# A decoder trunk step: weight preparation in spaced steps behind the evictions, rows transposed later, fourteen paired projections instead of thirteen

## The chip, the cores and the metric

The kernel runs on one NeuronCore of a Trainium2 chip. The core has five engines with queues of their own: TensorE (PE in the profile; its weight loads are PEld), VectorE (DVE), ScalarE (ACT), GpSimd (POOL) and SyncE (SP, which here only issues DMAs). The metric is the device time of one execution in microseconds (us); the median of three runs stands for a kernel.

## The reference

One layer of a decoder for a prompt of 1024 tokens and 32 sample tokens (8 sequences of 4), all in float32, model width 1024:

```python
h = layer_norm(ALPHA * x + 0.5 * swiglu(x, f1_w1, f1_w3, f1_w2), ln1_g, ln1_b)
z = h @ w_in + b_in                       # 42 blocks of 128 columns
# 18 blocks q, k, v of three attention groups; 8 blocks u, v of the gMLP; 16 blocks of gates gA, gB
att = combine_groups(...)                 # dilated sliding-window attention, prompt and sample
yb  = u * (tril(W_s) @ LN(v) + b)         # gMLP in chunks of 128
mix = (sigmoid(ga) * (att @ w_oa) + sigmoid(gb) * (yb @ w_ob)) @ w_out
h = layer_norm(ALPHA * h + mix, ln2_g, ln2_b)
h = layer_norm(ALPHA * h + 0.5 * swiglu(h, f2_w1, f2_w3, f2_w2), ln3_g, ln3_b)
```

The sample group also reads a stored key/value state of each window, and the shifted states are outputs.

## The kernel before

**Tiling.** The 1056 tokens lie along the free dimension in four chunks of 264 (C = 264, NC = 4), the 1024 features along eight blocks of 128 partitions. Each float32 operand is split into two parts of a faster format (fp32r): `split` (L253, L254) casts the value to a high part on ACT and subtracts it on DVE for the low part. A product of two such operands is three matmuls (`mm3`, L242): high by high, high by low, low by high. Every matmul of the main work multiplies a 128x128 weight block with 264 columns.

**Plain products and pairs.** A block of 128 output columns can be computed plainly: for one chunk `dense8` runs 8 x 3 = 24 matmuls into one PSUM bank. A gate done so is four calls of `gate8`. Two output blocks can instead be computed together by `pair` with a scheme of seven half-size products (Strassen's, in Winograd's form): the tokens and the features are halved, sums and differences of the input halves are built once by `spread`, and sums of the weight halves are built for each pair by `prep`. Each of the seven products is 24 matmuls over two PSUM banks; they run in the order 1, 2, 6, 7, 5, 4, 3 (called p1, p2, p6, p7, p5, p4, p3 here). So a pair takes 168 matmuls where two plain blocks take 192. After each product its banks are evicted into an SBUF tile: the first contribution by ACT (`put`, L1034), later ones by DVE (`add`, L1043). Banks come back soon: `one` holds p1, then p6, p5 and p3; `three` holds p7, then p4; `two` holds p2.

The feed-forward layers use the same scheme (`hidden`), and their second matrix a scheme of the same seven products with three inner blocks (`seven`).

**Order of the projection stage.** `widen` computes 6 of the 16 gates plainly (NLEAD = 6; the first 3 chunk by chunk while the layer norm before them ends, 3 more afterwards) and then NZ = 13 pairs: nine of q, k, v and four of u, v. The last ten gates are computed in `mix`, beside the attention.

**Preparing a pair's weights** (`prep`, a generator in five steps). Step 1 loads the two weight blocks (`ab`, L376, and `cd`, L377) on SP and splits `ab`. Step 2 builds s12, two sums, on POOL (L386, L387). Step 3 splits s12 into `h12`, `l12` and begins s34 (L392). Step 4 ends s34 (L394) and splits the quarter `dd` of `cd`. Step 5 splits s34. p1 and p2 use `ab`, p6 and p5 use s12, p7 and p3 use s34, p4 uses `dd`. The raw tiles R and the sums Q have two buffers each, so that a load waits for the readers of the pair before. While pair f runs, each product is followed by one step of prep(f+1) and by a `tick`.

**Ticks.** A tick advances generators of background work: three steps of the queue `bg`, one of `slow` (the sample attention, `sample`, and the input sums), three of `mid`. `sample_rows` is in `bg`: after four pauses it transposes on PE the sample tokens of the q, k, v pair before (L1375), copies them by DVE (L1377) and writes them by SP (L1381, L1386). `sample` streams the stored keys and values through three buffers (`M<-kv`, L1406) and multiplies and reduces them on DVE (L1421, L1422, L1432, L1437).

**Who sets the order.** The code is traced once and a list scheduler, with its own estimate of times, then decides each engine's order; each engine runs its list strictly in that order and waits at its head. `urgent` raises the priority of evictions and remembers the last one of each engine; `fenced` makes what is traced under it come after that one on DVE, ACT and SP. Background steps are fenced; the steps of `prep` are not:

```python
            def between():
                if f + 1 in preps:
                    next(preps[f + 1], None)
                self.tick(STEPS["strassen"], 1)
```

Of the kernel before, what the change touches and what calls it, by code (L numbers as in the profile page):

```python
# [59 lines left out]
REST = 3  # L60
GAP = 4
AFTER = 100
LATE = 16
MID = 3
HOP = (4, 1, 4)
# [3 lines left out]
FENCED = (mybir.EngineType.DVE, mybir.EngineType.Activation, mybir.EngineType.SP)  # L69
QKV = [s * 6 + 2 * g + hp for hp, g in HPG for s in range(3)]  # L70
GATES = [*range(34, 42), *range(26, 34)]
NLEAD = 6
NTAIL = 10
LAST = 3
EARLY = 6
BESIDE = {2: 13, 4: 14, 5: 15}
CHUNKED = 3
SPLIT = [*QKV, 22, 23, 24, 25, 18, 19, 20, 21, *GATES[NLEAD : 16 - NTAIL]]
DENSE = GATES[:NLEAD] + GATES[16 - NTAIL :]
# [4 lines left out]
class Trunk:  # L84
# [285 lines left out]
    def prep(self, src, f, H, engine):  # L370

        nc = self.nc
        lo, hi, n = slice(0, H), slice(H, 2 * H), 2 * H
        with self.tc.high_priority(offset=URGENT):
            ab, cd = self.R([P, D])[:, :n], self.R([P, D])[:, :n]
            nc.sync.dma_start(ab, src[1])  # L376
            dma = nc.sync.dma_start(cd, src[0])  # L377
        self.copy_state(dma, 2)
        tt = engine.tensor_tensor
        ah, al = self.W([P, D]), self.W([P, D])  # L380
        self.split(ah[:, :n], al[:, :n], ab)
        if f == LASTW2:
            h34, l34 = self.held([P, D], F32R), self.held([P, D], F32R)
        yield
        s12 = self.Q([P, D])
        tt(s12[:, lo], cd[:, lo], cd[:, hi], op=ALU.add)  # L386
        tt(s12[:, hi], s12[:, lo], ab[:, lo], op=ALU.subtract)  # L387
        yield
        s34 = self.Q([P, D])
        h12, l12 = self.W([P, D]), self.W([P, D])  # L390
        self.split(h12[:, :n], l12[:, :n], s12[:, :n])
        tt(s34[:, lo], ab[:, lo], cd[:, lo], op=ALU.subtract)  # L392
        yield
        tt(s34[:, hi], ab[:, hi], s12[:, hi], op=ALU.subtract)  # L394
        part = lambda h, l, o=0: [((h, l), o + k * P) for k in range(H // P)]
        if n == D:
            dd = self.S([P, D], F32R)
            self.split(dd[:, lo], dd[:, hi], cd[:, hi])
            p4 = part(dd[:, lo], dd[:, hi])
        else:  # L400
            p4 = []
            for h, l, w in ((ah, al, D - n), (h12, l12, H - (D - n))):
                o = H + len(p4) * P
                self.split(h[:, n : n + w], l[:, n : n + w], cd[:, o : o + w])
                p4 += part(h, l, n)[: w // P]
        yield
        if f != LASTW2:
            h34, l34 = self.S([P, D], F32R), self.S([P, D], F32R)
        self.split(h34[:, :n], l34[:, :n], s34[:, :n])
        self.L[f] = {  # L410
            1: part(ah, al), 2: part(ah, al, H), 5: part(h12, l12), 6: part(h12, l12, H),
            7: part(h34, l34), 3: part(h34, l34, H), 4: p4,
        }
        yield

    def product(self, t, p, f, first):
        while any(p not in t for t in self.T):
# [257 lines left out]
    def ffn(self, w13, w2p, w2, i, mode, resid):  # L675
        nc, preps = self.nc, {}
        plain = PLAIN[: 1 if i == 0 else 2]
        blocks = [f for f in range(FB) if f not in plain] + [FB + g for g in range(NG * (KB // 2))]
        after = dict(zip(blocks, blocks[1:]))

        def begin(f):
            if f < FB:
                preps[f] = self.prep(w13[f], f, KH * P, nc.gpsimd if f > 2 else nc.vector)
            else:
                preps[f] = self.prep(w2p[f - FB], f, HP, nc.vector)
            next(preps[f])

        if i == 0:
            self.lns = {}
            self.T, self.L = ({}, {}), {}  # L690
            units = self.lead_in(w13)
            self.new_x(1)
            self.consts()
            s0, s1 = (self.spread(j, self.Y, self.A, self.nc.vector) for j in range(2))
            begin(1)
            with self.tc.high_priority(offset=URGENT):
                for k in range(2):
                    self.load_x(self.nc.sync, 3, k, 0, KH)
            for c, work in enumerate((((2,), s0, s0, 1), ((3,), s0, 1, 1), (s1, s1, s1, 1), (1, s0))):
                self.hidden8(units, 0, c)  # L700
                for x in work:
                    if isinstance(x, tuple):
                        self.new_x(*x)
                    else:
                        next(preps[x] if x == 1 else x, None)
            self.bg.extend((s0, s1))
        else:
            lead, s1 = self.early
            lns, self.lns = self.lns, {}
            self.drain(lns[NC - 2])  # L710
            self.step(self.bg, 1)
            begin(1)
            for c in range(NC):
                self.drain(lns.pop(c))
                if c == NC - 1:
                    self.bg.append(s1)
                    self.step(self.bg, 2)
                for f, u in zip(plain, lead):
                    self.hidden8(u, f, c)
                    if c:  # L720
                        with self.chained():
                            next(preps[1], None)
            lead = self.early = None
        self.sqs = {}
        self.Y = self.A = None
        loads = deque(self.load_sums(resid))
        total = len(loads)

        def ready(f):
            for _ in preps.pop(f):  # L730
                pass
            if f in after:
                begin(after[f])

        def between(f, bg, slow=0):
            if after.get(f) in preps:
                next(preps[after[f]], None)
            self.tick(bg, slow)

        def load(n):  # L740

            with self.tc.high_priority(offset=URGENT):
                while loads and total - len(loads) < n:
                    loads.popleft()()

        for f in blocks[: FB - len(plain)]:
            ready(f)
            if f == FB - 1:
                load(2)
            count = iter(range(1, 8))  # L750

            def step():
                between(f, STEPS["strassen"])
                if f == FB - 1:
                    load(min(HEAD, 2 + 4 * next(count)))

            self.hidden(f, step)
            del self.L[f]
        self.T = ({}, {})
        self.normed = [None] * NC  # L760
        self.out(w2, i, mode, ready, between, load)
# [325 lines left out]
    def widen(self):  # L1087
# [29 lines left out]
        for n in range(CHUNKED, NLEAD):  # L1117
# [3 lines left out]
            for c in (1, 3, 0, 2):  # L1121
                self.gate8(w, DENSE[n], c, AF.Sigmoid, STEPS["lead"], 1)
                if n == NLEAD - 1:
                    next(preps[0], None)
        self.A = None
        for f in range(NZ):
            for _ in preps.pop(f):
# [2 lines left out]
                begin(f + 1)  # L1130

            def between():
                if f + 1 in preps:
                    next(preps[f + 1], None)
                self.tick(STEPS["strassen"], 1)

            self.pair(f, between)
# [231 lines left out]

    def sample_rows(self, *blocks):  # L1370
        nc, a = self.nc, self.a
        yield from self.pause(4)
        p = self.ax_tile()[:NS, : 2 * P].rearrange("p (s x) -> p s x", s=2)
        for x, (_, t) in enumerate(blocks):
            nc.tensor.transpose(p[:, x], t[:, NP:], self.ident)  # L1375
# [533 lines left out]
```

## Time and profile before

| | |
|---|---|
| median of 3 runs | 2154.41 us (2153.32 to 2157.72) |
| the profiled execution's own time | 2154.51 us |
| its span, first to last instruction | 2152.5 us |
| PE busy | 2122.6 us (99%), 17307 matmuls |
| DVE / ACT / POOL busy | 1549.5 (72%) / 889.4 (41%) / 317.1 us (15%) |
| DMA | 426.51 MB, 198 GB/s over the span |
| mean granted TensorE clock | 0.994 |

PE is the engine that is always busy, so the time is the sum of PE's work and of PE's waits. The stages along the span are: first feed-forward layer to about 660 us, its layer norm and the plain gates to about 787 us, the thirteen pairs to 1059 us, `mix` with the attention to about 1480 us, the second feed-forward layer to the end. A busy PE is modelled from pipelined matmuls; the granted clock is a share of 2.4 GHz (0.50 is 1.2 GHz).

### The profile page before, as it was taken

To read this page: it belongs to the slowest core of one execution; us is meant where nothing else is said; L and a number is where in the kernel's file an instruction comes from. 1 tells how busy PE (TensorE), PEld (TensorE's weight loads), DVE (VectorE), ACT (ScalarE), POOL (GpSimd) and SP (SyncE) were. 2 spreads that over 40 slices of the span, in tenths; PEclk is the share of its full clock that TensorE was granted. 3 is DMA by queue.
4 is the path that set the end of the run, shared out by engine and by line. 5 is a ranking of instruction groups with operands and counts; after the bars stand their busy time and mean duration, and the time that the engine had idled before them with its cause. 6 is when DMAs were issued, how large, how long until landed. Compare 5 with 4: busy or idle time off the path is not lost.

```text
span 2152.5 us, 43254 instructions
## 1 busy us (share of the span) xinstructions
PE 2122.6 (99%) x17307; PEld 2085.6 (97%) x17307; DVE 1549.5 (72%) x2727; ACT 889.4 (41%) x1680; POOL 317.1 (15%) x249
## 2 busy tenths in 40 slices
PE   9999999999999999999999999999999999999997
PEld 8999999999999999999988889999999999999997
DVE  8877767747789834777767758787667777657887
ACT  5444444422124634333476544164444444421224
POOL 0432322200000011323000000000323323100000
PEclk9999999999999999999999999999999999999998
DMA  4444555598885335676865765423454554596852
GB/s 155 145 140 170 183 166 168 189 338 315 327 325 176 130 103 177 201 231 198 296 211 187 223 190 177 154 110 110 144 174 156 183 173 153 194 408 267 311 186 81
DMA packets 168377, 426.51 MB, mean 198 GB/s; under 512 B 24352, under 2 KB 59792, under 8 KB 165488
## 3 DMA queue, kind: packets, MB, share of 16 engines
q1 hardware_dynamic: 167744, 423.21, 56.4%
q8 instruction: 135, 2.21, 0.4%
q10 hardware_dynamic: 432, 0.54, 0.1%
q14 instruction: 66, 0.54, 0.1%
HBM read 304.31 MB, written 165.57 MB: 218 GB/s over the span
## 4 chain that ended last, share of the span: by engine, by line
PE 89%; DVE 4%; DMA 4%; POOL 1%; issue 1%; ACT 0%; SPq 0%; ACTq 0%; DVEq 0%; POOLq 0%
PE ax L242 46%; PE mm L242 39%; DMA R<-wz 1%; PE ax L1206 1%; DMA M<-kv 1%; DMA S<-cD 1%; PE ax L1255 1%; PE ax L1232 1%; DVE W L254 1%; DMA S<-hD 0%; DVE S L632 0%; POOL Q L392 0%; POOL Q L387 0%; DVE S L254 0%; PE ax L621 0%
## 5 line engine op out<-in xcount | busy, mean ns | idle before, releaser
L242 PE MATMUL mm<-S,W 128*128 128x264 f32 x5400 | 713.6, 287 | 8.0 <-ACT S L253 2.3
L242 PE MATMUL ax<-S,W 128*128 128x264 f32 x5400 | 708.6, 285 | 1.3 <-ACT S L1034 1.1
L242 PEld LDWEIGHTS mm<-S,W 128*128 128x128 f32 x5400 | 677.1, 189 | 21.0 <-issue 7.0
L242 PEld LDWEIGHTS ax<-S,W 128*128 128x128 f32 x5400 | 678.5, 189 | 4.0 <-ACT S L1034 2.4
L242 PE MATMUL ax<-S,S 128*128 128x264 f32 x3240 | 475.9, 284 | 1.0 <-ACT S L1034 0.5
L242 PEld LDWEIGHTS ax<-S,S 128*128 128x128 f32 x3240 | 427.7, 188 | 1.7 <-DVE S L1043 0.9
L242 PE MATMUL mm<-S,S 128*128 128x264 f32 x2280 | 359.4, 286 | 2.6 <-DVE S L925 2.6
L242 PEld LDWEIGHTS mm<-S,S 128*128 128x128 f32 x2280 | 311.0, 189 | 3.9 <-issue 2.9
L253 ACT CAST W<-R 128x256 fp32r<-128x256 f32 (+2 forms) x175 | 130.6, 764 | 307.5 <-PE mm L242 139.9
L386 POOL TENSOR_TENSOR Q<-R 128x512 f32<-128x512 f32 x49 | 68.1, 1390 | 800.8 <-DMA R<-w13a 198.2
L254 DVE TENSOR_TENSOR W<-R,W 128x256 fp32r<-128x256 f32 (+2 forms) x175 | 154.6, 887 | 23.3 <-ACT W L253 21.7
L253 ACT CAST W<-Q 128x1024 fp32r<-128x1024 f32 (+1 forms) x78 | 76.8, 984 | 217.2 <-POOL Q L387 88.1
L820 DVE SCALAR_TENSOR_TENSOR S<-ax,S 128x264 f32<-128x264 f32 x240 | 99.7, 429 | 66.1 <-PE ax L242 65.7
L462 DVE TENSOR_TENSOR S<-ax,M 128x264 f32<-128x264 f32 x82 | 32.6, 433 | 144.7 <-PE ax L242 144.7
L254 DVE TENSOR_TENSOR S<-Q,S 128x1024 fp32r<-128x1024 f32 (+1 forms) x78 | 113.6, 1456 | 5.5 <-ACT S L253 5.4
L110 POOL CAST S<-ones 128x1 fp32r<-128x1 f32 x36 | 12.5, 355 | 675.7 <-PE ax L242 226.0
L254 DVE TENSOR_TENSOR W<-Q,W 128x1024 fp32r<-128x1024 f32 (+1 forms) x78 | 90.6, 1161 | 29.6 <-ACT W L253 29.6
L253 ACT CAST S<-Q 128x1024 fp32r<-128x1024 f32 (+1 forms) x78 | 76.7, 984 | 68.4 <-PE ax L242 49.8
L254 DVE TENSOR_TENSOR S<-S,M 128x528 fp32r<-128x528 f32 x72 | 84.6, 1175 | 2.5 <-ACT M L253 0.7
L253 ACT CAST S<-R 128x512 fp32r<-128x512 f32 (+1 forms) x62 | 42.0, 677 | 98.9 <-DMA sumsA<-S 40.6
L387 POOL TENSOR_TENSOR Q<-Q,R 128x512 f32<-128x512 f32 x49 | 81.0, 1653 | 2.7
L394 POOL TENSOR_TENSOR Q<-R,Q 128x512 f32<-128x512 f32 x49 | 79.7, 1627 | 1.2
(209 smaller groups left out, 2042.5 us busy)
## 6 DMA issues: line engine op xcount, KB each, us to landing
ws<-st SPq DMA_DIRECT2D x144, 256.0 KB
S<-sumsA SPq DMA_DIRECT2D x63, 528.0 KB
S<-sumsB SPq DMA_DIRECT2D x63, 528.0 KB
M<-kv SPq DMA_DIRECT2D x96, 256.0 KB
sumsA<-M SPq DMA_DIRECT2D x90, 264.0 KB
sumsB<-M SPq DMA_DIRECT2D x90, 264.0 KB
R<-w13b SPq DMA_DIRECT2D x44, 512.0 KB
R<-w13a SPq DMA_DIRECT2D x42, 512.0 KB
```

The source lines that it names most:

```text
L110: self.nc.gpsimd.tensor_copy(t[:, 0, :1] if len(shape) == 3 else t[:, :1], self.ones[:, :1])
L242: mm = lambda a, b, s, e: nc.tensor.matmul(o, a[:, cc], b, start=s, stop=e, skip_group_check=True)
L253: a = self.nc.scalar.copy(hi, src)
L254: b = self.nc.vector.tensor_tensor(lo, src, hi.bitcast(F32), op=ALU.subtract)
L386: tt(s12[:, lo], cd[:, lo], cd[:, hi], op=ALU.add)
L387: tt(s12[:, hi], s12[:, lo], ab[:, lo], op=ALU.subtract)
L394: tt(s34[:, hi], ab[:, hi], s12[:, hi], op=ALU.subtract)
L462: go(one, 5, False, lambda x: tt(h[:, x, 1], one[x], p7[:, x], op=ALU.add))
L820: nc.vector.scalar_tensor_tensor(y(x, r, e), bank[x], HALF, y(x, r, e), op0=ALU.mult, op1=ALU.add)
L1206: m = nc.tensor.matmul(pS[h][:, r, :nk], q[e, i * P : (i + 1) * P], k[e, k0 : k0 + nk], start=True, stop=True)
L1232: nc.tensor.transpose(pT[r][:, h, o], s[:, r, h, o], self.ident)
L1255: nc.tensor.matmul(pv[0][e, (i % 4) * P : (i % 4 + 1) * P], V[:, i - (nb - 1) + b, e], sT[:, r, h, b * P : b * P + P], start=b == 0, stop= ...
```

## The change

NLEAD goes from 6 to 4: two gates (blocks 38 and 39) are no longer computed plainly in `widen` but make a fourteenth pair after the u, v pairs; BESIDE, which names three of the gates left for `mix` by their place in the list, moves by two accordingly. In `prep` the split of `ab` goes from step 1 to step 2, the split of s12 from step 3 to step 4, and the two halves of s34 stand in steps 3 and 4. All steps of `prep` between products are now fenced (`advance`), in the pairs as in the feed-forward layers. `sample_rows` pauses for eight steps instead of four.

```diff
@@ -60,6 +60,7 @@
 REST = 3
 GAP = 4
 AFTER = 100
+ROWS = 8
 LATE = 16
 MID = 3
 HOP = (4, 1, 4)
@@ -69,11 +70,11 @@
 FENCED = (mybir.EngineType.DVE, mybir.EngineType.Activation, mybir.EngineType.SP)
 QKV = [s * 6 + 2 * g + hp for hp, g in HPG for s in range(3)]
 GATES = [*range(34, 42), *range(26, 34)]
-NLEAD = 6
+NLEAD = 4
 NTAIL = 10
 LAST = 3
 EARLY = 6
-BESIDE = {2: 13, 4: 14, 5: 15}
+BESIDE = {2: 11, 4: 12, 5: 13}
 CHUNKED = 3
 SPLIT = [*QKV, 22, 23, 24, 25, 18, 19, 20, 21, *GATES[NLEAD : 16 - NTAIL]]
 DENSE = GATES[:NLEAD] + GATES[16 - NTAIL :]
@@ -377,20 +378,20 @@
             dma = nc.sync.dma_start(cd, src[0])
         self.copy_state(dma, 2)
         tt = engine.tensor_tensor
-        ah, al = self.W([P, D]), self.W([P, D])
-        self.split(ah[:, :n], al[:, :n], ab)
         if f == LASTW2:
             h34, l34 = self.held([P, D], F32R), self.held([P, D], F32R)
         yield
         s12 = self.Q([P, D])
         tt(s12[:, lo], cd[:, lo], cd[:, hi], op=ALU.add)
         tt(s12[:, hi], s12[:, lo], ab[:, lo], op=ALU.subtract)
+        ah, al = self.W([P, D]), self.W([P, D])
+        self.split(ah[:, :n], al[:, :n], ab)
         yield
         s34 = self.Q([P, D])
+        tt(s34[:, lo], ab[:, lo], cd[:, lo], op=ALU.subtract)
+        yield
         h12, l12 = self.W([P, D]), self.W([P, D])
         self.split(h12[:, :n], l12[:, :n], s12[:, :n])
-        tt(s34[:, lo], ab[:, lo], cd[:, lo], op=ALU.subtract)
-        yield
         tt(s34[:, hi], ab[:, hi], s12[:, hi], op=ALU.subtract)
         part = lambda h, l, o=0: [((h, l), o + k * P) for k in range(H // P)]
         if n == D:
@@ -412,6 +413,11 @@
             7: part(h34, l34), 3: part(h34, l34, H), 4: p4,
         }
         yield
+
+    def advance(self, gen):
+        if gen is not None:
+            with self.fenced():
+                next(gen, None)
 
     def product(self, t, p, f, first):
         while any(p not in t for t in self.T):
@@ -733,8 +739,7 @@
                 begin(after[f])
 
         def between(f, bg, slow=0):
-            if after.get(f) in preps:
-                next(preps[after[f]], None)
+            self.advance(preps.get(after.get(f)))
             self.tick(bg, slow)
 
         def load(n):
@@ -1121,7 +1126,8 @@
             for c in (1, 3, 0, 2):
                 self.gate8(w, DENSE[n], c, AF.Sigmoid, STEPS["lead"], 1)
                 if n == NLEAD - 1:
-                    next(preps[0], None)
+                    for _ in range(2 if c == 2 else 1):
+                        next(preps[0], None)
         self.A = None
         for f in range(NZ):
             for _ in preps.pop(f):
@@ -1130,8 +1136,7 @@
                 begin(f + 1)
 
             def between():
-                if f + 1 in preps:
-                    next(preps[f + 1], None)
+                self.advance(preps.get(f + 1))
                 self.tick(STEPS["strassen"], 1)
 
             self.pair(f, between)
@@ -1369,7 +1374,7 @@
 
     def sample_rows(self, *blocks):
         nc, a = self.nc, self.a
-        yield from self.pause(4)
+        yield from self.pause(ROWS)
         p = self.ax_tile()[:NS, : 2 * P].rearrange("p (s x) -> p s x", s=2)
         for x, (_, t) in enumerate(blocks):
             nc.tensor.transpose(p[:, x], t[:, NP:], self.ident)
```

How this moves work in the projection stage is shown at three places. The pairs are counted from 0; in the names, W is a split weight, R a raw load, Q a sum, S a tile of inputs or results, ax and mm are PSUM banks.

The first place is ACT's list around the split of s12 for pair 7 (the cast to W1258 from Q1255 before, to W1237 from Q1231 after). Before, from the end of p7 of pair 5 (the first row) over p3 of pair 5 (S1232) to the first eviction of p1 of pair 6 (S1253):

```order
L1034 ACTIVATE S1233_10701<-ax1231_10699,cols_169 128x32
L1427 ACT_TABLE_LOAD
L1427 ACTIVATE X1188_10226,X1189_10229<-X1188_10226,X1189_10229 128x132
L253 CAST W1258_11021<-Q1255_10984 128x1024
L1034 ACTIVATE S1232_10700<-ax1226_10694,cols_169 128x66x4
L1034 ACTIVATE S1232_10700<-ax1227_10695,cols_169 128x58x4
L1034 ACTIVATE S1232_10700<-ax1227_10695,cols_169 128x32
L1034 ACTIVATE S1253_10954<-ax1247_10948,qb_171 128x16x16
```

The same split now, from the split of `ab` for pair 7 after p1 of pair 6, over the evictions of p6 of pair 6 (the first four rows of S1230) to the first eviction of p7:

```order
L254 CAST W1232_10745<-R1221_10700 128x1024
L1039 ACTIVATE S1230_10713<-ax1223_10706,cols_169 128x16x16
L1039 ACTIVATE S1230_10713<-ax1223_10706,cols_169 128x8
L1039 ACTIVATE S1230_10713<-ax1224_10707,cols_169 128x16x16
L1039 ACTIVATE S1230_10713<-ax1224_10707,cols_169 128x8
L254 CAST W1237_10817<-Q1231_10742 128x1024
L254 CAST S1239_10822<-R1222_10701 128x512
L1039 ACTIVATE S1230_10713<-mm1227_10710,cols_169 128x16x16
```

So the split of s12 for pair 7 stood ahead of the evictions of p3 of pair 5; now it stands behind those of p6 of pair 6, three products later, with the split of `dd` right behind it.

The second place is PE's list around the transposes of the sample rows. Before, in pair 6, between the last matmuls of p2 (mm1250) and the first of p6 (ax1247):

```order
L242 MATMUL mm1250_10951<-S975_8279,W1224_10690 128x264
L242 MATMUL mm1250_10951<-S974_8277,W1225_10691 128x264
L1375 MATMUL ax1260_11026<-ident_158,S1232_10700 32x128
L1375 MATMUL ax1260_11026<-ident_158,S1233_10701 32x128
L242 MATMUL ax1247_10948<-S1028_8763,W1236_10761 128x264
```

Now, in pair 6, between the last matmuls of p6 (ax1224) and the first of p7 (mm1227):

```order
L243 MATMUL ax1224_10707<-S1062_9071,W1214_10554 128x264
L243 MATMUL ax1224_10707<-S1058_9039,W1215_10555 128x264
L1380 MATMUL ax1240_10825<-ident_158,S1208_10458 32x128
L1380 MATMUL ax1240_10825<-ident_158,S1209_10459 32x128
L243 MATMUL mm1227_10710<-S1033_8797,S1219_10600 128x264
```

The transposes of pair 5's rows moved behind one more product.

The third place is SP's list in pair 5, around the second weight load of pair 7 (`cd`, R1244 before, R1222 after) and the writes of pair 4's sample rows (sD). Before:

```order
L1381 DMA sD_8628<-M1239_10769 32x2x64
L1386 DMA ws0<-M1239_10769 8x4x128
L1381 DMA sD_8628<-M1239_10769 32x2x64
L1410 DMA M1196_10272<-sD_8628 64x1x256 x2
L1406 DMA M1197_10273<-kv 128x512
L1394 DMA X1320_11615<-sD_8628 64x64
L377 DMA R1244_10939<-wz7 128x1024
```

Now:

```order
L1415 DMA M1170_10021<-sD_8628 64x1x256 x2
L1411 DMA M1171_10022<-kv 128x512
L1386 DMA sD_8628<-M1218_10565 32x2x64
L1391 DMA ws0<-M1218_10565 8x4x128
L1386 DMA sD_8628<-M1218_10565 32x2x64
L378 DMA R1222_10701<-wz7 128x1024
```

The load stays behind the writes of the sample rows, which themselves now follow p6 of the pair instead of p2.

## Rows read from the trace of the kernel before

**Rows 1.** The page: busy us (share) xinstructions of each engine.
```profile
PE 2122.6 (99%) x17307; PEld 2085.6 (97%) x17307; DVE 1549.5 (72%) x2727; ACT 889.4 (41%) x1680; POOL 317.1 (15%) x249
```
**Rows 2.** Windows: us, busy us PE PEld DVE ACT POOL, PEclk, DMA share, GB/s.
```profile
100.00:460.00 360.00, 360.00 (x2957) 360.00 (x2956) 253.38 (x345) 151.08 (x269) 100.11 (x64) 1.00 0.53 180
806.74:889.39 82.65, 82.65 (x682) 82.55 (x681) 48.67 (x80) 30.88 (x62) 20.33 (x15) 1.00 0.55 188
889.39:1020.26 130.87, 127.56 (x1020) 125.22 (x1019) 100.76 (x172) 52.29 (x102) 36.77 (x26) 0.99 0.66 214
1020.26:1040.68 20.42, 20.42 (x170) 20.42 (x169) 16.31 (x30) 12.99 (x24) 0.90 (x1) 1.00 0.71 236
```
**Rows 3.** The chain that ended last, at the gates: start us, us, what.
```profile
742.84 46.57 PE mm L242 x384
```
**Rows 4.** Waits of PE from 790 to 1062 us: total us, times, longest.
```profile
PE ax L1375 <- ACT S L1034: 1.7, 2, 1.2
PE ax L242 <- ACT S L1034: 1.6, 4, 0.6
PE ax L242 <- DVE S L1043: 0.4, 1, 0.4
```
**Rows 5.** Timeline of PE, pairs 5 to 7: start us, us, what [idle before].
```profile
889.39 3.11 PE L242 MATMUL mm<-S,W 128*128 128x264 f32 x24
910.36 3.07 PE L242 MATMUL mm<-S,W 128*128 128x264 f32 x24
...
913.96 0.39 PE L1375 MATMUL ax<-ident,S 128*32 128x128 f32 x2 [0.53 <-ACT S L1034]
914.59 3.44 PE L242 MATMUL ax<-S,W 128*128 128x264 f32 x24 [0.23 <-ACT S L1034]
...
937.75 0.40 PE L1375 MATMUL ax<-ident,S 128*32 128x128 f32 x2 [1.21 <-ACT S L1034]
```
**Rows 6.** Timeline of ACT, start of pairs 6 and 7.
```profile
911.75 1.05 ACT L253 CAST W<-Q 128x1024 fp32r<-128x1024 f32 x1 [4.89 <-POOL Q L387]
912.71 1.20 ACT L1034 ACTIVATE S<-ax,cols 128x264 f32<-128x264 f32 x3
...
935.26 1.05 ACT L253 CAST W<-Q 128x1024 fp32r<-128x1024 f32 x1 [13.15 <-POOL Q L387]
```
**Rows 7.** Waits of ACT from 806.74 to 1020.26 us.
```profile
ACT W L253 <- POOL Q L387: 74.0, 10, 13.2
```
**Rows 8.** The chain that ended last, pairs 5 and 6: start us, us, what.
```profile
902.53 4.80 DMA R<-wz
907.50 1.28 POOL Q L386
908.78 1.70 POOL Q L392
910.47 1.25 POOL Q L387
...
924.98 4.69 DMA R<-wz
```
**Rows 9.** Windows of 3.4 us after the wait at 937 us.
```profile
939.63:943.05 3.42, 3.42 (x18) 3.42 (x17) 1.61 (x4) 1.21 (x2) 0.00 (x0) 0.50 0.94 300
943.05:946.46 3.41, 3.41 (x30) 3.41 (x29) 3.41 (x6) 2.67 (x6) 0.00 (x0) 1.00 0.21 72
```
**Rows 10.** Waits of DVE from 806.74 to 1020.26 us.
```profile
DVE M L1421 <- DMA M<-kv: 13.2, 7, 2.9
DVE M L1432 <- DMA M<-kv: 6.7, 7, 2.3
```
**Rows 11.** Timeline of ACT at a table load.
```profile
714.44 1.28 ACT L994 ACT_TABLE_LOAD   x1
715.74 0.48 ACT L994 ACTIVATE M<-mm,cols 128x264 f32<-128x264 f32 x1
```
**Rows 12.** Timeline of DVE: the last difference of `spread`.
```profile
758.98 1.26 DVE L348 TENSOR_TENSOR S<-S,S 128x1056 fp32r<-128x1056 f32 x1 [1.65 <-ACT S L343]
```
**Rows 13.** Waits of PE from 1200 to 1300 us, end of the attention.
```profile
PE mm L242 <- DVE S L1585: 1.7, 2, 1.3
PE mm L242 <- DVE S L254: 0.8, 1, 0.8
```

## The prediction

> **What bounds the kernel now.** I read the page's busy times first: PE is busy 2122.6 us, 99% of the span, and no other engine more than 72% [rows 1]. So the time is PE's work plus the little that PE waits, and an edit is worth something only if it takes matmuls away or takes away a wait of PE. Next I read windows of PE by stage. In the first feed-forward layer PE is busy 360.00 of 360 us: nothing can be gained there. Four pairs (1 to 4, each counted from its p2 to the next) take 82.65 us without a gap, 82.65 / 4 = 20.66 each, and the pair from 1020.26 on, which has no sample rows to transpose, takes 20.42. But the six pairs from 889.39 on (5 to 10) take 130.87 us, with PE busy 127.56 and its clock at 0.99 [rows 2]. Five of these six have transposes, so at the clean price they would take 5 x 20.66 + 20.42 = 123.7. **7.1 us are lost there.**
>
> Where they go, I read from PE's waits: 1.7 + 1.6 us are waits for evictions by ACT, 0.4 for one by DVE, seven waits in all [rows 4], against 130.87 - 127.56 = 3.3 idle by the window, so I count 3.3. After the long wait the clock falls: from 939.63 on 18 matmuls take the 3.42 us in which 30 are done right after, at a granted clock of 0.50 (1.2 GHz) and then 1.00 (2.4 GHz) [rows 9]. Twelve matmuls fewer, at 2.91 / 24 us each (below), are 1.5 us. The other 7.1 - 3.3 - 1.5 = 2.3 us lie between the recorded waits, about 0.35 for each of the seven, where PE starts again after a wait.
>
> The cause of the waits stands in ACT's rows. PE waits 0.53 and 0.23 us after the p2 that starts at 910.36, and 1.21 at 937.75 [rows 5]. Just before, ACT has stood idle for 4.89 and 13.15 us at a cast of a sum Q, and the evictions, already due, run right behind that cast (three at 912.71) [rows 6]. ACT waits for POOL at this cast ten times, 74.0 us in all [rows 7]. POOL is late because the load is: in pair 5 `cd` is issued at 902.53, travels 4.80 us, and then s12's first half, s34's first half and s12's second take 1.28 + 1.70 + 1.25 [rows 8], so that s12 is ready at 911.7. By the order, this cast stands ahead of p3's evictions, and p3 ends one product before 910.36, at about 907.5. So the sum is 4.2 us late there; in the next pair, with its cast at 935.26 and p3's end near 930.5, 4.7.
>
> **The change part by part.** *Gates for a pair.* Two gates are 8 calls of 24 matmuls. In the chain, 16 products at the gates take 46.57 us [rows 3], 2.91 each, so 8 x 2.91 = 23.28 go out and a pair of 20.42 (no sample rows) comes in: **-2.9 us.**
>
> *The split of s12 behind p6's evictions.* The cast moves three products later, 3 x 2.91 = 8.7 us. The load behind the sum moves too: on SP it stands behind the row writes, which come one product (2.9) later because the transposes do. So the sum is late by 4.2 + 2.9 = 7.1 to 7.6 against a place 8.7 later: 1.1 to 1.6 us to spare. Then no eviction stands behind a waiting cast, PE's waits for ACT go, and the fall of the clock, which comes only after the longest of them, goes as well. What stays of the 7.1 us is the wait for DVE, 0.4 and its 0.35. The lower bound of the return is 0 and the upper 7.1. I take nearly all, less one leftover wait like the longest, 1.2 us [rows 4], since 1.1 to 1.6 is little spare next to the 0.5 by which the two pairs differ: 7.1 - 0.8 - 1.2 = **-5.1 us.** POOL's own order of the four sums does not change.
>
> *Rows transposed one product later* costs PE nothing, the two small matmuls are the same; the later writes are counted above, and the shifted outputs have the rest of the attention to land. *Split of `ab` one step later, and fences in the feed-forward layers*: 0. The cover is PE's queue without a gap (360.00 of 360), beside DVE at 253, ACT at 151 and POOL at 100 [rows 2]; ready two products later is still before the next pair. If that cover were gone, each wait would cost what those of the pairs do, some 0.3 to 1.2 us. *An earlier start of the pairs*: pair 0 comes 23.3 us sooner. The last difference of `spread` ends at 760.24 [rows 12]; the product that reads it last, p4, comes at about 763.2 + 4 x 2.91 = 774.9, so 14 us remain: 0.
>
> *ACT's table loads.* The fenced order holds 19 instead of 16. One takes 1.28 us and the next activation starts 0.02 us after its end [rows 11]: 3 x 1.28 = 3.8 us on an ACT that is busy 52.29 of 130.87 [rows 2]: hidden, 0. The page "ScalarE: Activation LUTs" of the Trainium skill, section "What ACT_TABLE_LOAD costs", speaks against the change more strongly: it gives about 1283 ns for the load and some 1380 more for a drain, 2.66 us for each switch, which would be an estimated 8.0 us of ACT. The trace agrees on the load (1.28) and shows no drain behind it in this row; by either figure ACT has the room, and PE's sum stays as it is.
>
> *The end of the attention.* The extra pair carries seven steps of background work that `mix` had to do. There PE waits 1.7 + 0.8 us [rows 13]. This can ease by up to 1.7, or grow by as much since the steps beside the eight gate calls are gone; I take 0.
>
> **Sum.** The profiled execution took 2154.51 us, 0.1 above the median of the runs. 2154.5 - 2.9 - 5.1 = **2146.5 us.**
>
> **The rivals.** *One: the waits move.* With ACT's evictions free, another late thing is next: DVE waits 13.2 + 6.7 us for the stored keys and values [rows 10], with evictions of its own behind these, and one such wait already reaches PE (0.4). If as much as ACT gave back is lost there, only the pair remains: 2154.5 - 2.9 = 2151.6, within 0.2%. For it: DVE is busy 100.76 of 130.87 in this stage, ACT only 52.29 [rows 2], and the fences put DVE's halves of the splits behind evictions too. Against it: of 3.7 us of recorded waits only 0.4 are DVE's.
>
> *Two: the load is later still, slower.* If `cd` lands later than I work out, the cast waits behind p6's evictions. PE feels it only when the spare 1.3, then p7 itself (2.9, until its evictions queue), then p5 less an eviction (2.9 - 1.3 = 1.6; p7's banks are next written by p4) are used up: 5.8 us. Beyond that each us costs PE once in each of eight q, k, v pairs. At 2 us beyond, 2154.5 - 2.9 - 7.1 + 8 x 2 = 2160.5; it is slower than before by over 0.2% from 1.8 us beyond. For it: DMA is at 0.66 of its time in this stage and at 0.94 in a window of it [rows 2, 9]; the load, with 4.80 and 4.69 us, is no short one [rows 8]; and on SP it stands behind writes that wait for PE, DVE and a fence. Against it: a move of 2.9 us would have to become one of nearly 11.
>
> *Three: all of it comes back.* No wait is left and `mix` eases: 2154.5 - 2.9 - 7.1 - 1.7 = 2142.8.
>
> **How the numbers follow.** A measurement of this kernel tells a change from none at about 0.2%, 4.3 us: faster is under 2150.1, slower above 2158.7. I give my forecast 0.60, rival one 0.24, rival two 0.06, rival three 0.10. That makes faster 0.70, the same 0.24, slower 0.06. The forecast's own range runs from 2144.4 (the leftover wait and the DVE wait gone too) to 2149.5 (two fifths of the 5.1 returned). For 8 in 10 the range goes from 2143.0, nearly all of rival three, to 2152.5, which takes in rival one with 0.9 us for small waits; rival two is left out.
>
> **What the profile after should show.** *Gates:* 8 products fewer ahead of the pairs, p2 of pair 0 near 763, and fourteen pairs. *Split:* the cast of s12 follows p6's evictions and waits for POOL for a us or not at all; no eviction by ACT runs right behind a long idle; the waits of PE for ACT between 765 and 1060 are under 1 us in all; the clock is 1.00 through the pairs, and the six pairs that took 130.87 take 124 to 126. *Rows:* `cd` is issued some 3 us later within its pair. *Feed-forward:* both layers as long as before, within half a us. *Mix*, which keeps its ten gates: as long as before within 2 us.
>
> **What would make it wrong.** A `cd` load that comes 9 us or more later (casts that wait for POOL with evictions queued behind); waits of PE for DVE that grow to several us, with a second fall of the clock; or feed-forward layers that grow, since any fence that holds a split past its product costs PE there at once, and there are many more products there than in the pairs.

## The result, and the profile after

The changed kernel takes 2158.89 us (median of 22 runs, 2156.05 to 2163.74); the kernel before, run beside it, 2155.93 (22 runs). The ratio of the two is 1.0015 (95% interval 1.0008 to 1.0021): some 3 us slower, where 8 us faster was forecast. The execution that was profiled took 2163.0 us, 4.1 above its median, and 8.5 more than the one of before, so its differences below add up to 8.1 in the four stages and not to 3.

I cut both traces into the same four stages, each from one matmul to another (the 500th and the 5500th from the start, the 8807th, the 5307th and the last counted from the end), so that the 24 matmuls fewer fall into the second:

| us | first feed-forward layer | gates and pairs | mix | second layer |
|---|---|---|---|---|
| before | 618.87 | 372.53 | 429.68 | 652.20 |
| changed | 621.26 | 362.39 | 436.99 | 660.71 |
| difference | +2.4 | -10.1 | +7.3 | +8.5 |

The gates and pairs gave 10.1 us, where 8.0 were forecast; it was lost again in three stages that the prediction had at nothing. The page of the changed kernel, first part, beside [rows 1]:

```profile
PE 2122.1 (98%) x17283; PEld 2087.1 (97%) x17283; DVE 1536.9 (71%) x2735; ACT 890.4 (41%) x1689; POOL 291.3 (13%) x253
```

**The pairs.** Windows of the changed kernel (us, busy us of PE, PEld, DVE, ACT, POOL, clock, DMA share, GB/s); the second is the six pairs 5 to 10, from p2 to p2, as in [rows 2]:

```profile
100.00:460.00 360.00, 360.00 (x2952) 360.00 (x2951) 238.26 (x340) 148.50 (x270) 86.64 (x64) 1.00 0.53 178
869.66:993.20 123.54, 123.54 (x1019) 123.41 (x1018) 104.95 (x173) 52.22 (x101) 37.41 (x25) 1.00 0.71 235
```

123.54 instead of 130.87, without an idle moment of PE and at full clock: 7.3 us back. ACT's timeline at pair 6, to be held against [rows 6], and POOL's ahead of it:

```profile
896.04 1.40 ACT L1039 ACTIVATE S<-ax,cols 128x256 f32<-128x256 f32 x4 [3.55 <-PE ax L243]
897.30 1.06 ACT L254 CAST W<-Q 128x1024 fp32r<-128x1024 f32 x1
```
```profile
884.38 1.30 POOL L385 TENSOR_TENSOR Q<-R 128x512 f32<-128x512 f32 x1 [13.72 <-DMA R<-wz]
885.62 1.37 POOL L391 TENSOR_TENSOR Q<-R,R 128x512 f32<-128x512 f32 x1
886.95 1.74 POOL L386 TENSOR_TENSOR Q<-Q,R 128x512 f32<-128x512 f32 x1
```

The cast of s12 runs right behind p6's evictions and waits for nothing; its sum was ready at 888.69 (886.95 + 1.74), 8.6 us before. The forecast had 1.1 to 1.6 to spare. It took the load to come 2.9 us later; in fact `cd` is issued at 880.77, 11.1 us after p2 of pair 5, where before it was 902.53 - 889.39 = 13.1 after it. One reason stands in the waits of SP's queue in pairs 1 to 10, before (first line) and changed:

```profile
SPq L1381 <- DVE M L1377: 32.9, 8, 5.6
```
```profile
SPq L1386 <- DVE M L1382: 5.1, 3, 3.0
```

Before, the row writes ahead of the load stood at SP's head for 32.9 us, waiting for the copy of the transposed rows, and these transposes were what waited for evictions behind the late cast. It looks like a circle: a late load makes a late sum, the cast holds the evictions, these the transposes, the writes and the next load. That the lateness fed itself so is argued from these waits, and the experiments show that the writes are not the main thing: in pairs_plain (below) SP stands at them only twice in pairs 1 to 10 (12.3 us), `cd` is issued 11.9 to 13.2 us after p2 in pairs 5 to 7 (before 13.1 to 14.6, changed 11.0 to 11.2), and ACT still waits 73.1 us for s12 there, where it had waited 74.0. The load differs by 1 to 3 us; what frees ACT is the place of the cast.

**The second feed-forward layer.** PE's longest new wait, in the timeline of PE, and the windows at and behind it:

```profile
1936.64 1.25 PE L243 MATMUL ax<-S,W 128*128 128x264 f32 x4 [4.17 <-ACT W L254]
```
```profile
1936.01:1942.84 6.83, 6.20 (x28) 6.20 (x29) 5.97 (x11) 2.75 (x5) 0.00 (x0) 0.50 0.29 83
1942.84:1949.67 6.83, 6.83 (x58) 6.83 (x58) 5.99 (x14) 3.12 (x5) 0.00 (x0) 1.00 1.00 353
```

4.17 us of wait, then 28 matmuls in the time of 58 at a clock of 0.50 (1.2 GHz). Counted matmul for matmul, the layer is level with before up to 1894 us and 8.3 us behind at 1952, so the whole loss lies here. ACT's timeline and the chain that ended last say for what:

```profile
1932.73 0.63 ACT L254 CAST M<-M 128x528 fp32r<-128x528 f32 x1 [18.56 <-DMA M<-hidB]
1935.76 1.49 ACT L254 CAST W<-R 128x768 fp32r<-128x768 f32 x3 [2.40 <-DMA R<-w2pb]
```
```profile
1928.23 7.43 DMA R<-w2pb
```

The split of `ab` for the third of the twelve units of `seven` in this layer follows a load that was issued at 1928.23 and took 7.43 us. SP's timeline shows why it was issued so late: the load, the fifth from w2pb in both kernels, has moved from ahead of the store of the last hidden block (hidB) and its read-backs (M from hidB: plain blocks, which are split and written to partB) to behind them, and is issued 25.5 us later. Before, left out what is not of these:

```profile
1902.72 0.33 SPq L376 DMA_DIRECT2D R<-w2pb  x1
...
1918.56 0.32 SPq L848 DMA_DIRECT2D M<-hidB  x1
...
1921.62 0.32 SPq L471 DMA_DIRECT2D hidB<-S  x1
1922.85 0.43 SPq L848 DMA_DIRECT2D M<-hidB  x1
1924.20 1.65 SPq L867 DMA_DIRECT2D partB<-M  x2
```

Changed:

```profile
1922.34 0.32 SPq L477 DMA_DIRECT2D hidB<-S  x1
1923.62 3.04 SPq L853 DMA_DIRECT2D M<-hidB  x3
1927.64 0.32 SPq L872 DMA_DIRECT2D partB<-M  x1
1928.23 0.45 SPq L377 DMA_DIRECT2D R<-w2pb  x1
```

**Mix.** PE's waits there in the changed kernel follow (zD holds the projected blocks in DRAM). Before had 6.0 us in all, with 1.9 the largest line:

```profile
PE mm L243 <- DVE S L1590: 4.3, 6, 1.8
PE ax L1211 <- DVE X L1221: 2.2, 1, 2.2
PE mm L243 <- DVE S L255: 1.9, 1, 1.9
PE ax L1211 <- DMA S<-zD: 1.9, 1, 1.9
PE mm L243 <- DVE S L1716: 0.6, 1, 0.6
PE mm L243 <- ACT W L254: 0.5, 1, 0.5
PE ax L1194 <- DMA S<-zD: 0.2, 1, 0.2
```

They are 11.6 us, and there are three stretches of 3.4 us at a clock of 0.50 that before has not. DVE's timeline shows the pattern, at 1195 and again at 1273:

```profile
1195.64 1.23 DVE L1370 TENSOR_TENSOR S<-S,S 128x1024 f32<-128x1024 f32 x1 [3.56 <-DMA S<-cD]
1196.78 0.28 DVE L1221 CUSTOM_DVE_ANT_0 S<-ax,S 128x128 f32<-128x128 f32 x1
...
1273.40 1.23 DVE L1370 TENSOR_TENSOR S<-S,S 128x1024 f32<-128x1024 f32 x1 [4.18 <-DMA S<-cD]
1274.54 0.76 DVE L1590 TENSOR_TENSOR S<-S,mm 128x264 f32<-128x264 f32 x2
```

DVE stands at a product that waits for coefficients to be read back from DRAM (cD), and the evictions that PE needs, of the scores (L1221) and of the projections (L1590), stand behind it. Before, DVE waits at both places too:

```profile
1207.81 1.23 DVE L1365 TENSOR_TENSOR S<-S,S 128x1024 f32<-128x1024 f32 x1 [2.94 <-DMA S<-cD]
1208.95 0.22 DVE L1438 TENSOR_TENSOR X<-X,X 128x64 f32<-128x64 f32 x1
...
1280.31 1.23 DVE L1365 TENSOR_TENSOR S<-S,S 128x1024 f32<-128x1024 f32 x1 [3.08 <-DMA S<-cD]
```

Its waits for cD are 7.8 us in all, against 11.4 now. What differs is above all what stands behind them: at 1207.81 a step of the sample attention (L1438) follows and no eviction of scores, since four of these had just run, from 1203.22 on. So the fault of the pairs, a waiting instruction ahead of evictions, appears on another engine.

### The profile page after: what moved, and what is told of

The parts are those of the page before. It is cut to its first block, busy times and chain, and to the rows that moved or that the text cites. A ratio compares the mean times of both kernels' runs of the same rounds, so it can differ in the third digit from the quotient of the medians.

```text
span 2161.2 us, 42820 instructions
## 1 busy us (share of the span) xinstructions
PE 2122.1 (98%) x17283; PEld 2087.1 (97%) x17283; DVE 1536.9 (71%) x2735; ACT 890.4 (41%) x1689; POOL 291.3 (13%) x253
## 4 chain that ended last, share of the span: by engine, by line
PE 92%; DVE 4%; DMA 3%; ACT 1%; issue 1%; SPq 0%; ACTq 0%; POOL 0%; DVEq 0%
PE ax L243 49%; PE mm L243 38%; DMA S<-cD 1%; PE ax L1211 1%; PE ax L1260 1%; PE ax L1237 1%; DVE S L638 1%; DVE W L255 1%; DMA S<-zD 0%; DVE S L255 0%; PE ax L627 0%; PE mm L1556 0%; DVE S L561 0%; DMA R<-w2pb 0%; DMA S<-xc 0%
## 5 line engine op out<-in xcount | busy, mean ns | idle before, releaser
L243 PE MATMUL ax<-S,W 128*128 128x264 f32 x5472 | 721.0, 285 | 6.2 <-ACT W L254 4.2
L243 PE MATMUL mm<-S,W 128*128 128x264 f32 x5232 | 694.8, 288 | 13.4 <-DVE S L1590 4.3
L243 PEld LDWEIGHTS mm<-S,W 128*128 128x128 f32 x5232 | 659.5, 190 | 25.3 <-DVE S L1590 6.2
L255 DVE TENSOR_TENSOR W<-R,W 128x1024 fp32r<-128x1024 f32 (+3 forms) x174 | 150.6, 872 | 113.2 <-ACT W L254 109.0
L254 ACT CAST W<-R 128x1024 fp32r<-128x1024 f32 (+3 forms) x174 | 130.1, 763 | 212.5 <-PE mm L243 66.0
L255 DVE TENSOR_TENSOR S<-Q,S 128x1024 fp32r<-128x1024 f32 (+1 forms) x79 | 90.3, 1143 | 50.9 <-ACT S L254 50.8
L472 ACT ACTIVATE S<-S 128x528 f32<-128x528 f32 x82 | 48.5, 638 | 169.7 <-DVE S L471 169.7
L473 DVE TENSOR_TENSOR S<-S,M 128x264 f32<-128x264 f32 x82 | 95.4, 1192 | 15.1 <-ACT S L472 14.2
L466 ACT COPY M<-ax 128x264 f32<-128x264 f32 x82 | 30.7, 380 | 134.6 <-PE ax L243 134.5
L464 ACT COPY M<-ax 128x264 f32<-128x264 f32 x82 | 28.9, 381 | 136.7 <-issue 93.1
L1039 ACT ACTIVATE S<-ax,cols 128x264 f32<-128x264 f32 (+5 forms) x99 | 40.4, 496 | 88.0 <-PE ax L243 83.6
```

The costliest lines, as they stand in the source:

```text
L243: mm = lambda a, b, s, e: nc.tensor.matmul(o, a[:, cc], b, start=s, stop=e, skip_group_check=True)
L254: a = self.nc.scalar.copy(hi, src)
L255: b = self.nc.vector.tensor_tensor(lo, src, hi.bitcast(F32), op=ALU.subtract)
L464: go(one, 1, True, lambda x: copy(r1[:, x], one[x]))
L466: go(one, 6, False, lambda x: copy(u2[:, x], one[x]))
L472: lambda x: nc.scalar.activation(h[:, x], h[:, x], AF.Silu),
```

## The experiments

Each kernel was timed in turns with the kernel before. "Against before" is the ratio with its 95% interval; the stages, in us, are those of the one profiled execution, as above, so a stage can stand several us off where that execution does.

| kernel | against before | layer 1 | gates, pairs | mix | layer 2 |
|---|---|---|---|---|---|
| changed | 1.0015 (1.0008 to 1.0021) | 621.26 | 362.39 | 436.99 | 660.71 |
| prep_pairs | 0.9976 (0.9967 to 0.9984) | 618.39 | 365.00 | 436.51 | 652.27 |
| pairs14 | 1.0019 (1.0010 to 1.0028) | 618.79 | 371.96 | 436.05 | 652.40 |
| prep_all | 1.0025 (1.0015 to 1.0034) | 621.18 | 365.55 | 429.83 | 659.83 |
| ffn_old | 0.9980 (0.9969 to 0.9990) | 618.39 | 361.79 | 433.87 | 652.42 |
| m_silent | 0.9954 (0.9941 to 0.9966) | 618.83 | 361.80 | 431.27 | 652.06 |
| ffn_plain | 0.9977 (0.9967 to 0.9986) | 618.76 | 361.79 | 434.59 | 652.42 |
| ffn_fence | 0.9992 (0.9984 to 1.0001) | 616.71 | 362.56 | 433.01 | 658.04 |
| ffn_old_rows4 | 0.9972 (0.9962 to 0.9981) | 618.79 | 362.04 | 434.05 | 652.43 |
| pairs_plain | 0.9976 (0.9967 to 0.9985) | 618.43 | 367.69 | 431.11 | 652.08 |
| pairs_fence_old | 0.9967 (0.9955 to 0.9979) | 618.41 | 365.23 | 431.79 | 652.07 |
| fence_w13 | 0.9979 (0.9970 to 0.9987) | 619.55 | 362.13 | 434.84 | 653.28 |
| m_silent2 | 1.0014 (1.0005 to 1.0023) | 618.77 | 361.77 | 444.69 | 652.46 |

The theory after the result: each part of the change acts in a stage of its own. The preparation frees the pairs; its fences cost the feed-forward layers; the moved gates cost mix. The first four kernels split these.

**prep_pairs**: the preparation in the pairs alone; against the changed kernel, with the old steps of `prep` for the feed-forward weights besides:

```diff
-NLEAD = 4
+NLEAD = 6
-ROWS = 8
+ROWS = 4
...
-            self.advance(preps.get(after.get(f)))
+            if after.get(f) in preps:
+                next(preps[after[f]], None)
```

> Kernel before with the spaced, fenced preparation in the pairs alone; feed-forward layers, gates (NLEAD 6, thirteen pairs) and the rows' pause as before. Theory (the three parts of the change act each in its own stage: the preparation returns the 7.1 us lost in the pairs; its fences cost the feed-forward layers; the moved gates cost mix): PE's waits for ACT in the pairs gone, all else as before, so 6 to 7.5 us faster than before (about 2149 against 2156). Rival (what the pairs return is lost behind them, because the attention is no further ahead when mix begins): 0 to 2 us faster.

5.2 us faster, by the interval 3.4 to 7.1. The pairs gained 7.5, both feed-forward layers stood as before. In the profiled run (5.2 above this kernel's median) mix is 6.8 longer: its first transposes waited 2.6 us for a read from zD and the clock fell there. The interval reaches into the theory's 6 to 7.5 and lies outside the rival's 0 to 2; whether a part of the gain is regularly lost again in mix, that one run does not show.

**pairs14**: NLEAD 4 and BESIDE on the kernel before, nothing else.

> Kernel before with NLEAD 4 and fourteen pairs alone; preparation, fences and the rows' pause as before. Theory: minus 2.9 us for the 24 matmuls, the pairs' 7.1 us of loss stay, and mix, whose order the moved gates alone change, is some 5 to 7.3 us longer: 2 to 4.5 us slower than before. Rival (mix is longer because the faster pairs reach it with less of the attention done, or only in the one profiled run): 2.9 us faster, with mix as long as before.

4.1 us slower: mix is 6.4 longer though no pair became clean, so it is not the earlier arrival. The gates and pairs, with 24 matmuls (2.9) fewer, are only 0.6 shorter, so its pairs lost more than those of before: PE waits 6.2 us for ACT there, against 3.3 [rows 4].

**prep_all**: preparation and fences everywhere, NLEAD 6, ROWS 4.

> Kernel before with the spaced, fenced preparation everywhere, pairs and feed-forward layers; NLEAD 6 and the rows' pause as before, so that mix has the order of before. Theory: 7.1 us returned in the pairs, 3 us lost in the first feed-forward layer and 2.5 to 8.7 in the second: between 4.6 slower and 1.6 faster, near no change; mix as before. Rival (the waits seen in the feed-forward layers belong to the one profiled run): 6 to 7 us faster.

5.4 us slower, a little beyond the theory's range, far from the rival. Mix is as before (429.83), and the wait of the second layer is there again, in the waits of PE:

```profile
PE ax L243 <- ACT W L254: 4.3, 1, 4.3
```

So it belongs to the kernel and not to one run.

**ffn_old**: the changed kernel, feed-forward preparation as before (the diff above without its first four lines, and the old steps there).

> The changed kernel with the preparation in the feed-forward layers as before (split of ab in step 1, no fence); all else as in the change: fourteen pairs, spaced and fenced preparation in the pairs, the later rows. Theory: the feed-forward layers as long as before, the pairs clean, only mix still longer by 5 to 7.3 us: minus 2.9 minus 7.1 plus 5 to 7.3, 3 to 5 us faster than before. Rival (the feed-forward waits are not the fences' doing): no faster than the changed kernel, 3 us slower than before.

4.3 us faster than before: as the theory had it. The feed-forward part costs about 1.0015 - 0.9980 = 0.0035 of 2155, 7.5 us.

Then the parts of the feed-forward loss. **ffn_plain** takes away the fence there and keeps the new steps; **ffn_fence** keeps the fence with the old steps; **fence_w13** keeps both, but the fence for the first matrices only:

```diff
-            self.advance(preps.get(after.get(f)))
+            if after.get(f, 0) < FB:
+                self.advance(preps.get(after.get(f)))
+            elif after[f] in preps:
+                next(preps[after[f]], None)
```

> The changed kernel with the fence alone taken from the preparation in the feed-forward layers; its new steps (split of ab in step 2, of s12 in step 4) stay. Theory (the fences take the lead that the preparation had over PE there; the steps do little): feed-forward layers as before, like ffn_old, about 5 us faster than before. Rival (the later steps are what costs): waits of PE at 1932 and the like stay, 3 us slower than before.

> The changed kernel with the old steps of the preparation in the feed-forward layers, but fenced there. Theory (the fences cost, the steps do little): the losses of the feed-forward layers stay for the larger part, 0 to 4 us slower than before. Rival (the later steps are what costs): like ffn_old, about 5 us faster than before.

> The changed kernel with the fence taken from the preparation of the second matrices (the scheme with three inner blocks) alone; the first matrices' preparation stays fenced, with the new steps. Theory (nearly all of the feed-forward loss lies where the second matrices' loads are put behind the stored hidden blocks and their read-back): 7 to 9 us faster than the changed kernel, 4 to 6 us faster than before, the wait at 1932 gone. Rival (both kinds of preparation lose by the fence alike): half of it, 0 to 2 us faster than before.

Without the fence the later steps cost nothing (5.0 us faster than before). With the fence and the old steps the kernel is 1.7 faster than before, within noise (0.9984 to 1.0001): better than its theory of 0 to 4 slower, and short of the rival's 5 faster. The second layer keeps 5.6 of its 8.3 us (658.04 and 660.71 against 652.42), the first loses nothing (616.71). So the fence alone costs some 3 us (0.9992 - 0.9977), the later steps alone nothing, and both together some 8 (1.0015 - 0.9977): the theory that the steps do little holds only where there is no fence. With the fence on the first matrices alone it is 4.5 faster than before and 7.8 faster than the changed kernel: nearly all of the loss was in the second matrices, as expected. The load's place agrees in each: in fence_w13 it is ahead of the store of the hidden block again and the wait of PE is gone; in ffn_fence it stands behind the store but ahead of the two writes to partB, and PE waits half as long:

```profile
PE ax L243 <- ACT W L254: 2.2, 1, 2.2
```

**ffn_old_rows4**: the rows' pause back at four.

> Like ffn_old, with the pause of the sample rows back at four steps. Theory (the later rows neither cost nor give on PE; the split of s12 behind the evictions of p6 has its slack either way): within 1.5 us of ffn_old, about 5 us faster than before. Rival (the earlier transposes wait for evictions again, as they did in the kernel before): waits of PE at the transposes, 2 to 4 us slower than ffn_old.

6.0 us faster than before, within the interval of ffn_old. The later transposes give nothing and cost nothing that shows; with a pause of four SP still waits 16.0 us for the copied rows in pairs 1 to 10, and neither ACT's cast nor PE waits for it.

Then mix. **m_silent** is ffn_old with no tick in the fourteenth pair; **m_silent2** (NZ - 2 for NZ - 1) leaves out those of the last two pairs:

```diff
-                self.tick(STEPS["strassen"], 1)
+                if f < NZ - 1:
+                    self.tick(STEPS["strassen"], 1)
```

> Like ffn_old (the change with the feed-forward layers' preparation as before), and in the fourteenth pair no tick: the seven steps of sample attention that the extra pair carried are left where they were before, and the order of mix comes near to that of before. Theory (mix is longer because the seven extra steps shift the sample attention against the rest of DVE's list there): mix as long as before, so minus 2.9 minus 7.1, 8 to 10 us faster than before, 3 to 6 faster than ffn_old. Rival (mix is longer because it starts earlier, whatever its order): like ffn_old, about 5 us faster than before.

> Like m_silent, but the last two pairs carry no tick, so that mix begins seven steps of sample attention behind the kernel before (where the changed kernel is seven ahead). Theory (mix is sensitive to any shift of the sample attention against DVE's other work, since its order was fitted to one alignment): mix 2 to 6 us longer than in m_silent, 4 to 8 us faster than before. Rival (the more of the sample attention runs ahead of mix, the longer mix is): as fast as m_silent or faster, 10 us or more faster than before.

m_silent (5 runs) is the fastest of all: 9.9 us faster than before, 5.6 faster than ffn_old (0.9980 - 0.9954; the two intervals do not meet). Its mix takes 431.27 with 8.5 us of waits, and no fall of the clock. The waits for the projections on DVE are back near those of before (first line m_silent, second before; the changed kernel had 4.3, 6, 1.8):

```profile
PE mm L243 <- DVE S L1609: 2.4, 3, 1.2
PE mm L242 <- DVE S L1585: 1.9, 3, 1.3
```

m_silent2 loses all of that: 3.0 slower than before, mix 13.4 longer than m_silent's, more than twice what was expected. There the end of the sample attention is late, and PE waits for its join:

```profile
PE ax L1495 <- DVE X L1492: 6.6, 1, 6.6
PE mm L243 <- DVE S L1609: 5.2, 6, 2.1
```

So it is neither the earlier start of mix nor "the more ahead, the worse": seven steps of the sample attention too many or too few at the start of mix both cost, by different waits.

Last, the parts of the gain, on m_silent. **pairs_plain** has the new steps without the fence in the pairs; **pairs_fence_old** the fence with the old steps:

```diff
-                self.advance(preps.get(f + 1))
+                if f + 1 in preps:
+                    next(preps[f + 1], None)
```

> Like m_silent, but the preparation in the pairs without the fence, its new steps kept. In ACT's list the cast of s12 then stands ahead of p3's evictions of the pair before, as in the kernel before, while the load behind it comes later by the later rows. Theory (what frees the pairs is the place of that cast behind evictions that come first, and here the fence sets it): the pairs lose 7 us or more again, waits of PE for ACT return, 7 to 14 us slower than m_silent, 0 to 3 us faster or slightly slower than before. Rival (the later steps alone do it): within 1.5 us of m_silent, about 10 us faster than before.

> Like m_silent, but the old steps of the preparation in the pairs, with the fence. The cast of s12 then stands behind p2's evictions, ahead of p6's, one product earlier than in the change. Theory (the fence does it, the step adds slack that is used in part): the sum is ready at about the time of that place (7.1 to 7.6 us late against a place 5.8 later), so a wait of 1 to 2 us per pair ahead of p6's evictions, which PE feels little: 0 to 4 us slower than m_silent. Rival (the step is needed as well): 7 us slower than m_silent, the pairs as long as before.

pairs_plain has ACT's old wait again, longer than in [rows 7] (from 765 to 1060 us):

```profile
ACT W L254 <- POOL Q L387: 90.6, 13, 11.5
```

and loses 4.7 us to m_silent (0.9976 - 0.9954), less than the 7 to 14 expected: PE's waits come to 3.7 us and this time the clock did not fall. The new steps alone do not free the pairs. pairs_fence_old loses 2.8, the size that the theory gave, but not by its wait: the cast of s12 waits for POOL only once from 765 to 1060 us (3.9 us), while the split of `ab` now waits nine times for its load:

```profile
ACT W L254 <- DMA R<-wz: 26.9, 9, 6.6
```

By the stage of gates and pairs, the old preparation takes 371.96 (pairs14), the new steps alone 367.69, the fence alone 365.23 and both 361.80 (m_silent). So the fence does the larger part and the later step the rest; by the ratios alone pairs_plain and pairs_fence_old are not told apart, since their intervals overlap.

## Why the prediction was wrong

**Gates for a pair, -2.9: right.** Gates and pairs are 2.6 us shorter in the changed kernel than with the same preparation in the pairs and thirteen of them (365.00 - 362.39).

**The split of s12, -5.1: right in kind, too small.** 7.3 came back, the upper bound of 7.1 and more. The leftover wait of 1.2 and the 0.8 of DVE's did not occur. The load, forecast some 3 us later in its pair, came 2.0 us earlier (11.1 for 13.1): I had moved the load with the row writes, and not seen that these writes were themselves late behind the cast (32.9 us of SP's waits; 16.0 with the old pause in ffn_old_rows4, 5.1 in the changed kernel). In the pairs it came out as rival three has it, and rival two fell; they look as described (cast behind p6's evictions, no wait of PE for ACT, clock 1.00, 123.54 us against 124 to 126).

**Rows, table loads, earlier pairs: 0, right.** With a pause of four the time is the same; ACT was busy 890.4 us with the three more loads (889.4 before), and no wait of PE in the pairs is for it.

**The step that failed: "Split of `ab` one step later, and fences in the feed-forward layers: 0".** In place of 0 it measured +2.4 and +8.5 us in the stages, 7.5 (ffn_old) to 10.6 (prep_all against prep_pairs) in the ratios. I took as cover that PE's queue has no gap (360.00 of 360 [rows 2]) and that the other engines are not full. Both are still so after the change in the same window (360.00 of 360), and the loss lies elsewhere, at the seam between the layer's first and second matrices, where the hidden blocks are stored, read back and split. No row of that place stood in the prediction. The fence took the lead that the unfenced preparation had: the same split of `ab` ran at 1922.79 before and runs at 1935.76 now, PE idle. That the scheduler puts the load behind the store because the raw tiles come free later in its estimate is argued; that its place goes with the wait is shown by fence_w13 and ffn_fence: no such wait with the load ahead of the store, 2.2 us with it between the store and the writes to partB, 4.2 behind the first of these writes. The cover that the prediction gave second, "ready two products later is still before the next pair", failed with it: the split ran 13.0 us later, where two products of a pair are 5.8. The first layer's 2.4 is not taken apart further: 0.4 us of it are spread over the steady stretch up to 376 us, 2.2 come between there and 614, with 1.4 us of waits for a split (the longest 1.0, at 606), and its cause stays open. The prediction named all this as what would make it wrong ("any fence that holds a split past its product costs PE there at once"); it gave it no chance, and a price of 0.3 to 1.2 us for each wait, taken from the pairs, where the one wait at 1932 was 4.17 and brought a fall of the clock.

**The second term that failed: "The end of the attention ... I take 0", with bounds of 1.7.** It measured +7.3 in the profiled execution, which lies 4.1 above its kernel's median, and 5.6 between ffn_old and m_silent. I bounded it by PE's waits at one place [rows 13], whereas the seven steps shift the sample attention against all of DVE's list from 1190 to 1300. The waits after it are of the kind that I had found on ACT and did not look for on DVE.

**Rival one** (only the pair remains, 2151.6) was nearest by its kind, waits that move elsewhere, but not by its place: DVE's waits for keys and values in pairs 1 to 10 fell from 19.9 us [rows 10] to 1.5. No rival had a loss outside the pairs.

## What to carry to other kernels

A fence or a later step that frees one stage should be tried in that stage alone: here it cost run-ahead where the preparation had to be early, and the place was not the steady stretch but the seam, where a load, a store and its read-back share a queue. Read each queue's list for what stands ahead of the moved instruction there, not only how full its engine is. And where parts of a kernel carry background work, check at which point they hand it on: here seven steps more and seven fewer both cost. m_silent, with the fence in the pairs alone and the extra pair silent, keeps both gains and is 9.9 us faster than before.

## What the runs showed of the hardware

A short wait of PE costs more than itself when the clock falls after it. The 4.17 us at 1932 were followed by 6.83 us at 0.50 (1.2 GHz). The last 0.63 us of the wait lie in that window; in the other 6.20 us 28 matmuls ran, which take 28 x 6.83 / 58 = 3.3 us at the clock of the window behind it (1.00): some 2.9 us more. The clock fell behind single waits of 1.21 us [rows 4, 9], 1.92 and 2.20 us, and did not behind 1.2 in pairs_plain, 1.6 in m_silent or 2.49 in pairs14. A wait of 1.90 us at the first layer norm (near 665 us) is the same in four of the kernels; behind it the clock fell in the kernel before and in m_silent, and did not in ffn_old and pairs_plain. So the length of the wait alone does not tell.

A load of 128x768 took 7.43 us while the DMA engines were busy 0.95 of the time, against 4.69 to 4.80 for the larger 128x1024 of the pairs [rows 8], where they were busy 0.66 of it over the six pairs [rows 2]:

```profile
1928.23:1935.66 7.43, 4.25 (x35) 4.03 (x34) 2.79 (x7) 0.63 (x1) 0.00 (x0) 1.00 0.95 371
```

One execution can stand 4 to 5 us off its kernel's median (the changed kernel by 4.1, prep_pairs by 5.2), more than the result itself.
